# Start addresses of the activation tiles in the three-pass products of a hybrid decoder layer

## The chip, the cores and the metric

The kernel runs on one core of one Trainium2 chip. The metric is device time in microseconds (us) for one execution. Three runs of the kernel before gave 1511.25, 1512.42 and 1514.81 us; the median is 1512.42 us.

## The reference

One decoder layer for 256 tokens of width 2048, all in float32. Cut to what the kernel spends its time on:

```python
h = rms_norm(x, ln1)
proj = h @ w_in                      # 2048 -> 12304 columns: GDN q|k|v, beta, decay, out-gate z,
                                     # MoBA q|k|v, gate A, gate B
y_a = gated_deltanet(...) @ w_branch_a          # 8 heads of 128, chunked delta rule
y_b = moba_attention(q_b, k_b, v_b) @ w_branch_b
merged = sigmoid(gate_a) * y_a + sigmoid(gate_b) * y_b
x = x + merged @ w_out               # 2048 x 2048
h = rms_norm(x, ln2)
u = causal_dwconv(h @ w_up) + bias   # 2048 x 11264
u_gate, u_val = split(u)
x = x + (silu(u_gate) * u_val) @ w_down         # 5632 x 2048
return rms_norm(x, final_norm)
```

## The kernel before

**Three passes.** Every large product is taken in the float32r type, and to keep float32 accuracy each operand is split into a rounded high part and a low rest (`split`, L117 and `low`, L114: ScalarE casts the high part, VectorE subtracts to get the low one). A product is then high x high, plus high x low, plus low x high. The weights come from HBM one 128 x 2048 block at a time (`load_w`), land in `wraw` and are split into `wh` and `wl`, two buffers of each.

**The activation tiles.** For all products but the last the activations are transposed, 128 partitions by 16 (or 8) blocks of the contraction by 256 tokens, and the high and low parts lie side by side in one tile with the shape [128, blocks, 2, 256]:

- `hc` (L220): the normalised input, for the input projection. It stays until the end of the gates; `h2` and `tail` later take the same place in memory (their `tag` is "hc").
- `yca`, `ycb` (L707): the two branches' outputs, 8 blocks each.
- `mc` (L716): the merged branches, for the output projection.
- `h2` (L739): the second normalised input, for the up projection.
- `tail` (L797): no activations; the split weights of the last two blocks of the down projection.

**How they are read.** In `block` (L164 on) TensorE holds 128 columns of `wh` or `wl` and streams the activation tile past them. In wide form, used from the fifth gate chunk on (`WIDE_AT = 4`), one contraction block takes two matmuls, because the high and the low part are read as one row of 512:

```python
main_mm(ps, wh[:, k, :], x[:, k], k == 0, False)                          # 512 columns
main_mm(ps[:, 0, :], wl[:, k, :], x[:, k, 0, :], False, k == kt - 1)      # 256 columns
```

Before that, in narrow form, it takes three matmuls of 256 columns: two with `wh`, one with `wl`. Narrow are the chunks called `gdn`, `z` and `moba` and the first four of `gate`; wide are the other twelve of `gate`, and `br` (from `yca`, `ycb`), `wo` (from `mc`) and `up` (from `h2`). The value projection `ps_v` is the other way round: `hc` is held, in pieces of 128, and 512 columns of `wh` or `wl` stream past. The down projection (`pd`) holds the split activations `ah`, `al` and streams 512 columns of `wh`, `wl` or, for its last two blocks, `tail`. The small product `ps_bd` holds 48 columns of `wb2` and streams `hc`.

**Order.** The Tile framework's scheduler sets the order on each engine when the program is built; weights are loaded on the SP queue, up to four blocks ahead.

**Where the tiles start.** A tile pool gives out addresses in steps of 32 bytes in each partition. In the program that is built, the weights `wh`, `wl` and the activations `ah`, `al` start at a multiple of 64 bytes, and so does `mc`; `hc`, `h2`, `tail`, `yca`, `ycb` and `wb2` start 32 bytes behind one. The rows and pieces within a tile are 512, 1024 or 2048 bytes apart, so that every matmul of a tile starts at the tile's own place.

Of the kernel before, what the change touches and what calls it, by code (L numbers as in the profile page):

```python
# [12 lines left out]
F32R = mybir.dt.float32r  # L13
# [6 lines left out]
P = 128  # L20
T = 256
D = 2048
KD = D // P
H = 8
# [56 lines left out]
def layer_kernel(ctx: ExitStack, tc: tile.TileContext, xT, pos, cst, csel, ceye, vec, convw, ffw, bdv,  # L81
# [7 lines left out]

    def r3(t, b):  # L90
        return t.rearrange("p (a b) -> p a b", b=b)

    def mmg(ps, pairs, start=True, stop=True, **kw):
        n = len(pairs)
        for i, (a, b) in enumerate(pairs):
            pe.matmul(ps, a, b, start=(start and i == 0), stop=(stop and i == n - 1), **kw)  # L96
# [17 lines left out]
    def low(hi, lo, src, eng=None):  # L114
        (eng or dve).tensor_tensor(lo, src, hi.bitcast(F32), op=ALU.subtract)  # L115
# [48 lines left out]
    def block(ps, w, x, kt, k0=0, k1=None):  # L164
        wh, wl = (r3(t, P) for t in w)
        for k in range(k0, k1 or kt):
            if len(ps.shape) == 2:
                for w_, a in ((wh, 0), (wh, 1), (wl, 0)):
                    main_mm(ps, w_[:, k, :], x[:, k, a, :], k == 0 and w_ is wh and a == 0,
                            k == kt - 1 and w_ is wl)  # L170
                continue
            main_mm(ps, wh[:, k, :], x[:, k], k == 0, False)
            main_mm(ps[:, 0, :], wl[:, k, :], x[:, k, 0, :], False, k == kt - 1)
# [43 lines left out]

    hst = ExitStack()
    hp = hst.enter_context(tc.tile_pool(name="hp", bufs=1, side="right"))
    hc = hp.tile([P, KD, 2, T], F32R, name="hc", tag="hc")  # L220
    hh, hl = hc[:, :, 0, :], hc[:, :, 1, :]
    front = ExitStack()
    fk = front.enter_context(tc.tile_pool(name="fk", bufs=1))
# [16 lines left out]
    for i in range(4):  # L240
        scaled(xs[:, 4 * i:4 * i + 4, :], ln1v, 4 * i, hh, hl)
        for b in range(2):
            raw, wh, wl = (t[:, 512 * i:512 * i + 512] for t in wq[b])
            split(wh, wl, raw)
            for k in range(4):
                a = 4 * i + k
                main_mm(ps_q0[:, b], r3(wh, P)[:, k], hh[:, a], a == b == 0, False)
                main_mm(ps_q0[:, b], r3(wh, P)[:, k], hl[:, a], False, False)
                main_mm(ps_q0[:, b], r3(wl, P)[:, k], hh[:, a], False, a == KD - 1)
# [94 lines left out]
    m = m_st.enter_context(tc.tile_pool(name="m", bufs=2, reuse_waits="tile"))  # L344
# [315 lines left out]
    for gr in range(4):  # L660
        h0 = 2 * gr
        qk = []
        for a in range(2):
            ps = chunk(pair(w_moba, 2 * gr + a), hc, KD, "moba")
            t = m.tile([P, 2, T], F32, name=f"qk{a}")
            join(t, ps, R1b)
            qk.append(t)
        if gr % 2 == 0:
            ps = [mmt("ps_v").rearrange("p a b -> p (a b)") for _ in range(2)]
            for q_ in range(4):  # L670
                wh, wl = (r3(t, 512) for t in load_w(w_mv[2 * gr + q_]))
                for i in range(2):
                    s = slice(i * P, (i + 1) * P)
                    for k in range(4):
                        a = q_ * 4 + k
# [28 lines left out]
    yp = y_st.enter_context(tc.tile_pool(name="yp", bufs=1, side="right", reuse_waits="tile"))  # L704
    yc = []
    for t, nm_ in ((ya, "a"), (yb, "b")):
        yc.append(yp.tile([P, H, 2, T], F32R, name="yc" + nm_))  # L707
        for i in range(4):
            s = slice(2 * i, 2 * i + 2)
            act.copy(yc[-1][:, s, 0, :], t[:, s])  # L710
            low(yc[-1][:, s, 0, :], yc[-1][:, s, 1, :], t[:, s], pool)
# [1 line left out]

    m_st = ExitStack()
    m = m_st.enter_context(tc.tile_pool(name="mp", bufs=1, reuse_waits="tile"))
    mc = m.tile([P, KD, 2, T], F32R, name="mc")  # L716
    for c in range(8):
        bts = [yp.tile([P, 2, T], F32, name="bt", bufs=3) for _ in range(2)]
        join(bts[0], chunk(pair(w_ba, c), yc[0], H, "br"), gts[:, c])
# [16 lines left out]
    b = bp.enter_context(tc.tile_pool(name="b", bufs=2, reuse_waits="tile"))  # L736
    x1 = bkeep.tile([P, KD, T], F32, name="x1")
    sqa = b.tile([P, 2, T], F32, name="sqa", bufs=1)
    h2 = hp.tile([P, KD, 2, T], F32R, name="h2", tag="hc")  # L739
    for c in range(8):  # L740
        steps = ((0, 0, KD - 2), (1, 0, 8), (0, KD - 2, KD), (1, 8, KD))
        ps = chunk(pair(w_o, c), mc, KD, "wo", **({} if c else dict(piece=512, steps=steps)))
# [19 lines left out]
    b = bk.enter_context(tc.tile_pool(name="b2", bufs=2, reuse_waits="tile"))  # L762
    ak = bk.enter_context(tc.tile_pool(name="ak", bufs=1, side="right", reuse_waits="tile"))
    acts = ak.tile([P, NF, T], F32, name="acts")
    for c in range(NF):
# [3 lines left out]
        t = b.tile([P, 2, T], F32, name="cvf")  # L769
# [24 lines left out]

    LAST = 4
    wl = {}
    tail = hp.tile([P, 2, 2, 2048], F32R, name="tail", tag="hc")  # L797

    def down(i, n, k, stop=False):
        ah, al, wh, wl_ = wl[k]  # L800
# [105 lines left out]
```

## Time and profile before

| what | us |
|---|---|
| median of three runs | 1512.42 |
| the profiled execution | 1512.97 |
| its span, first to last instruction | 1510.8 |
| TensorE busy | 1487.7 (98%) |
| VectorE busy | 1027.2 (68%) |
| ScalarE busy | 754.6 (50%) |
| up projection, its piece of the chain that ended last | 483.3 |

The profile is one execution. The chain of work that ended last is followed back from the last instruction: its shares say which engine and which line set the end. A matmul's own duration is no measure of pace, since matmuls overlap in the engine's pipeline: the pace is read from the starts of successive matmuls, or from a piece of the chain that is nothing but matmuls, by its length and its count. Below, the pitch is the time from one start to the next. Some matmul records can be missing from a trace, so a count is taken from a short piece where it can be.

### The profile page before, as it was taken

What the parts mean: (1) busy time and instruction counts of PE and PEld (TensorE: products, weight loads), DVE (VectorE), ACT (ScalarE), POOL (GpSimd) and SP (SyncE); (2) the same over time, 40 slices, a digit from 0 to 9 for tenths busy, and PEclk for the clock granted to TensorE, in tenths of its full rate; (3) what the DMA queues carried; (4) which work ended last, traced back from release to release, by engine and by line L of the source; (5) the groups of instructions that cost most, each with busy time, mean ns of one, the idle gap of its engine ahead of it and who ended that gap; (6) DMA issues with size and microseconds to landing.
All of it is one profiled execution on the core that took longest, in us unless ns stands there. A gap on an engine that the chain in (4) does not pass through costs nothing.

```text
span 1510.8 us, 22511 instructions
## 1 busy us (share of the span) xinstructions
PE 1487.7 (98%) x9179; PEld 1337.7 (89%) x9179; DVE 1027.2 (68%) x1453; ACT 754.6 (50%) x1026; POOL 184.9 (12%) x137
## 2 busy tenths in 40 slices
PE   7999999999999999999999999999999999999997
PEld 6999999998998888888888888888888888888886
DVE  7898785886765555777767767667676676555554
ACT  5664464434474444545455555555555554444444
POOL 3001101141221000110101111211111110000000
PEclk9999999999999999999999999999999999999999
DMA  9454444444336553568545555555555554555552
GB/s 312 156 191 165 167 148 171 154 150 165 140 116 219 193 183 126 173 219 307 194 169 195 195 189 190 181 192 196 190 190 181 193 195 167 195 195 195 195 195 84
DMA packets 45639, 276.94 MB, mean 183 GB/s; under 512 B 5504, under 2 KB 6992, under 8 KB 15456
## 3 DMA queue, kind: packets, MB, share of 16 engines
q1 hardware_dynamic: 43712, 270.98, 50.0%
q0 software_dynamic: 960, 2.36, 0.5%
q10 hardware_dynamic: 864, 2.16, 0.4%
q8 instruction: 72, 1.18, 0.3%
q14 instruction: 31, 0.25, 0.0%
HBM read 271.68 MB, written 3.80 MB: 182 GB/s over the span
## 4 chain that ended last, share of the span: by engine, by line
PE 93%; DVE 4%; ACT 1%; issue 1%; DMA 0%; POOL 0%; SPq 0%; DVEq 0%; ACTq 0%
PE ps_up L108 32%; PE pd L96 16%; PE ps_gate L108 11%; PE ps_gdn L108 9%; PE ps_wo L108 6%; PE ps_br L108 5%; PE ps_moba L108 4%; PE ps_z L108 3%; PE ps_v L108 3%; DVE wl L115 2%; ACT wh L118 1%; PE g L96 1%; PE py L545 1%; PE pu L551 1%; DMA wraw<-in_w_gdn 0%
## 5 line engine op out<-in xcount | busy, mean ns | idle before, releaser
L115 DVE TENSOR_TENSOR wl<-wraw,wh 128x1024 fp32r<-128x1024 f32 (+1 forms) x508 | 611.8, 1237 | 255.5 <-ACT wh L118 254.2
L118 ACT CAST wh<-wraw 128x1024 fp32r<-128x1024 f32 (+1 forms) x508 | 502.3, 1033 | 379.3 <-PE ps_up L108 117.5
L108 PE MATMUL ps_up<-h,wh 128*128 128x512 f32 x1408 | 488.6, 390 | 0.0
L108 PE MATMUL ps_up<-h,wl 128*128 128x256 f32 x1408 | 397.0, 282 | 0.0
L108 PEld LDWEIGHTS ps_up<-h,wh 128*128 128x128 f32 x1408 | 264.4, 188 | 55.4
L108 PEld LDWEIGHTS ps_up<-h,wl 128*128 128x128 f32 x1408 | 266.1, 189 | 0.1
L108 PE MATMUL ps_gate<-hc,wh 128*128 128x512 f32 (+1 forms) x640 | 179.6, 347 | 0.0
L108 PE MATMUL ps_gdn<-hc,wh 128*128 128x256 f32 x768 | 143.7, 287 | 8.9 <-ACT wh L118 6.2
L108 PE MATMUL ps_gate<-hc,wl 128*128 128x256 f32 x512 | 144.6, 282 | 0.8 <-DVE wl L115 0.8
L778 POOL TENSOR_TENSOR acts<-sg,cvf 128x256 f32<-128x256 f32 x44 | 80.8, 1836 | 423.3 <-ACT sg L777 423.3
L108 PEld LDWEIGHTS ps_gdn<-hc,wh 128*128 128x128 f32 x768 | 122.1, 194 | 10.3 <-ACT wh L118 6.5
L96 PE MATMUL pd<-wl,ah 128*128 128x512 f32 x336 | 130.8, 389 | 0.0
L96 PE MATMUL pd<-wh,al 128*128 128x512 f32 x336 | 130.8, 389 | 0.0
L108 PEld LDWEIGHTS ps_gate<-hc,wh 128*128 128x128 f32 x640 | 111.4, 188 | 15.1
L108 PE MATMUL ps_gdn<-hc,wl 128*128 128x256 f32 x384 | 110.5, 288 | 1.1 <-DVE wl L115 1.1
L772 ACT ACTIVATE cvf<-unf,ffv 128x256 f32<-128x256 f32 x88 | 48.2, 595 | 104.5 <-DVE unf L199 104.5
L774 DVE SCALAR_TENSOR_TENSOR cvf<-unf,ffv,cvf 128x254 f32<-128x254 f32 (+1 forms) x176 | 77.3, 481 | 32.1 <-ACT cvf L772 31.8
L108 PEld LDWEIGHTS ps_gate<-hc,wl 128*128 128x128 f32 x512 | 96.6, 189 | 1.0 <-DVE wl L115 1.0
L108 PE MATMUL ps_moba<-hc,wh 128*128 128x256 f32 x512 | 93.0, 282 | 0.0
L96 PE MATMUL pd<-wh,ah 128*128 128x512 f32 x336 | 92.8, 391 | 0.0
L108 PE MATMUL ps_wo<-mc,wh 128*128 128x512 f32 x256 | 88.8, 391 | 0.0
L118 ACT CAST ah<-acts 128x256 fp32r<-128x256 f32 x44 | 17.9, 407 | 125.8 <-PE pd L96 116.1
(426 smaller groups left out, 2061.9 us busy)
## 6 DMA issues: line engine op xcount, KB each, us to landing
wraw<-in_w_up SPq DMA_DIRECT2D x88, 1024.0 KB, 4.7
wraw<-in_w_dn SPq DMA_DIRECT2D x44, 1024.0 KB, 4.7
wraw<-in_w_gate SPq DMA_DIRECT2D x32, 1024.0 KB, 4.8
wraw<-in_w_gdn SPq DMA_DIRECT2D x30, 1024.0 KB, 4.8
wraw<-in_w_moba SPq DMA_DIRECT2D x16, 1024.0 KB, 4.8
wraw<-in_w_o SPq DMA_DIRECT2D x16, 1024.0 KB, 4.8
wraw<-in_w_mv SPq DMA_DIRECT2D x8, 1024.0 KB, 4.8
wraw<-in_w_ba SPq DMA_DIRECT2D x16, 512.0 KB, 3.4
```

What stands on the lines that cost most here:

```text
L96: pe.matmul(ps, a, b, start=(start and i == 0), stop=(stop and i == n - 1), **kw)
L108: pe.matmul(ps, a, b, start=start, stop=stop, skip_group_check=True)
L115: (eng or dve).tensor_tensor(lo, src, hi.bitcast(F32), op=ALU.subtract)
L118: act.copy(hi, src)
L545: pe.matmul(py[:, p], ats[p], Tm[:, p], start=True, stop=True)
L551: pe.matmul(pu[:, p], Y[:, p, :], odd(U)[:, p], start=True, stop=True)
L772: act.activation(t[:, j, :], un[:, j, :], AF.Identity, scale=w[:, 2:3], bias=w[:, 3:4])
L774: dve.scalar_tensor_tensor(t[:, j, d:], un[:, j, :T - d], w[:, 2 - d:3 - d], t[:, j, d:], op0=ALU.mult, op1=ALU.add)
L778: pool.tensor_tensor(acts[:, c, :], sg, t[:, 1, :], op=ALU.mult)
```

## The change

Each of the tiles is made 128 elements (512 bytes) longer, and the activations begin some elements into it, by a new helper:

```diff
+    def operand(tp, name, kt, off, tag=None):
+        t = tp.tile([P, kt * 2 * T + 128], F32R, name=name, tag=tag or name)
+        return t[:, off:off + kt * 2 * T].rearrange("p (k a t) -> p k a t", a=2, t=T)
...
-    hc = hp.tile([P, KD, 2, T], F32R, name="hc", tag="hc")
+    hc = operand(hp, "hc", KD, 8, "hc")
...
-        yc.append(yp.tile([P, H, 2, T], F32R, name="yc" + nm_))
+        yc.append(operand(yp, "yc" + nm_, H, 4 if nm_ == "a" else 32))
...
-    mc = m.tile([P, KD, 2, T], F32R, name="mc")
+    mc = operand(m, "mc", KD, 2)
...
-    h2 = hp.tile([P, KD, 2, T], F32R, name="h2", tag="hc")
+    h2 = operand(hp, "h2", KD, 12, "hc")
...
-    tail = hp.tile([P, 2, 2, 2048], F32R, name="tail", tag="hc")
+    tail = hp.tile([P, 2 * 2 * 2048 + 128], F32R, name="tail", tag="hc")[:, :8192].rearrange(
+        "p (a b c) -> p a b c", a=2, b=2)
```

Counted in the two built programs, the start of what the matmuls read, in bytes behind a multiple of 64:

| tile | before | changed | read by |
|---|---|---|---|
| `hc` | 32 | 0 | gdn, z, moba, gate (streamed), ps_v (held) |
| `yca` | 32 | 48 | br, first half |
| `ycb` | 32 | 32 | br, second half |
| `mc` | 0 | 8 | wo |
| `h2` | 32 | 16 | up |
| `tail` | 32 | 32 | pd, last two blocks |
| `wh`, `wl`, `ah`, `al` | 0 | 0 | everywhere |

Other tiles in the same pools move by multiples of 512 bytes and keep their place against 64. On all five engines the two programs hold the same instructions in the same order, with the same shapes and the same waits; no instruction is added, removed or moved.

## Rows read from the trace of the kernel before

**Rows 1.** Page, part 1: busy us, share of the span, instruction count.
```profile
PE 1487.7 (98%) x9179; PEld 1337.7 (89%) x9179; DVE 1027.2 (68%) x1453; ACT 754.6 (50%) x1026; POOL 184.9 (12%) x137
```
**Rows 2.** Chain that ended last: share of the span by engine, tile and line.
```profile
by line: PE ps_up L108 32.3%; PE pd L96 15.9%; PE ps_gate L108 11.1%; PE ps_gdn L108 8.8%; PE ps_wo L108 5.9%; PE ps_br L108 4.6%; PE ps_moba L108 3.9%; PE ps_z L108 3.0%; PE ps_v L108 3.0%; DVE wl L115 2.0%; issue 0.8%; ACT wh L118 0.7%; P
```
**Rows 3.** Stretches: us; busy PE, PEld, DVE, ACT, POOL; granted clock; DMA share; GB/s.
```profile
30.00:400.00 370.00, 367.97 (x2928) 356.33 (x2926) 292.01 (x564) 182.47 (x238) 57.52 (x57) 1.00 0.46 164
...
780.00:1258.00 478.00, 478.00 (x2759) 423.76 (x2759) 332.94 (x435) 251.74 (x349) 79.40 (x43) 1.00 0.53 190
```
**Rows 4.** Pieces of the chain in order of time: start us, us, what, count.
```profile
681.18 88.75 PE ps_wo L108 x512
...
776.52 483.26 PE ps_up L108 x2788
```
**Rows 5.** Timeline of TensorE, value projection: start us, us, matmul, count.
```profile
257.22 0.63 PE L108 MATMUL ps_v<-wh,hc 128*128 128x512 f32 x2
...
259.32 0.40 PE L108 MATMUL ps_v<-wh,hc 128*128 128x512 f32 x1
```
**Rows 6.** Timeline of TensorE, end of the down projection.
```profile
1486.31 1.52 PE L96 MATMUL pd<-wh,ah 128*128 128x512 f32 x6
1487.67 0.39 PE L96 MATMUL pd<-wl,ah 128*128 128x512 f32 x1
...
1489.52 0.39 PE L96 MATMUL pd<-wl,ah 128*128 128x512 f32 x1
...
1491.38 0.40 PE L96 MATMUL pd<-wl,ah 128*128 128x512 f32 x1
```
**Rows 7.** Pieces of the chain: narrow chunks, and the product with 48 held columns.
```profile
28.55 3.63 PE ps_bd L96 x32
...
105.33 11.20 PE ps_z L108 x96
...
327.39 8.63 PE ps_moba L108 x74
...
415.52 9.19 PE ps_gate L108 x78
```
**Rows 8.** Groups of matmuls by shape: count, busy us, mean ns of one.
```profile
L108 PE MATMUL ps_up<-h,wh 128*128 128x512 f32 x1408 | 488.6, 390 | 0.0
...
L108 PE MATMUL ps_gdn<-hc,wh 128*128 128x256 f32 x768 | 143.7, 287 | 8.9 <-ACT wh L118 6.2 <-DVE hc L204 2.6
...
L108 PE MATMUL ps_gate<-hc,wh 128*128 128x512 f32 x384 | 133.2, 390 | 0.0
...
L108 PE MATMUL ps_moba<-hc,wh 128*128 128x256 f32 x512 | 93.0, 282 | 0.0
...
L108 PE MATMUL ps_gate<-hc,wh 128*128 128x256 f32 x256 | 46.5, 282 | 0.0
L108 PE MATMUL ps_z<-hc,wh 128*128 128x256 f32 x256 | 45.9, 281 | 0.0
...
L108 PE MATMUL ps_br<-yca,wh 128*128 128x512 f32 x128 | 44.7, 390 | 0.0
...
L108 PE MATMUL ps_v<-wh,hc 128*128 128x512 f32 x128 | 41.1, 399 | 0.0
```
**Rows 9.** TensorE, start of the kernel: us, busy (count), granted clock, DMA share, GB/s.
```profile
20.00:23.00 3.00, 3.00 (x16) 0.50 0.93 329
```
**Rows 10.** Timeline of TensorE in that stretch.
```profile
22.42 0.63 PE L108 MATMUL ps_gdn<-hc,wh 128*128 128x256 f32 x2
...
23.06 0.63 PE L108 MATMUL ps_gdn<-hc,wh 128*128 128x256 f32 x2
```
**Rows 11.** VectorE groups of the first convolution: count, busy us, mean ns.
```profile
L420 DVE SCALAR_TENSOR_TENSOR kq<-un,cwv,kq 128x253 f32<-128x253 f32 x16 | 7.2, 472 | 0.0
L420 DVE SCALAR_TENSOR_TENSOR kq<-un,cwv,kq 128x255 f32<-128x255 f32 x16 | 7.1, 473 | 0.7 <-ACT kq L418 0.7
L420 DVE SCALAR_TENSOR_TENSOR kq<-un,cwv,kq 128x254 f32<-128x254 f32 x16 | 7.0, 473 | 0.0
```

## The prediction

> **What bounds the kernel now.** I read the busy shares first, then the chain that ended last, then the starts of single matmuls. TensorE is busy for 98% of the span [rows 1], and the chain is TensorE almost throughout: the up projection alone is 32.3% of it, the down projection 15.9%, the gates 11.1% [rows 2]. Over the up projection TensorE has no idle time at the full granted clock, 1.00, which is 2.4 GHz, while VectorE is busy for 333 of 478 us, ScalarE for 252, and the DMA engines for 53% [rows 3]. So in the long stages the end is set by the pitch of the matmuls, and whatever the change does to the pitch passes into the time in full, in both directions: the feeding engines have a quarter or more to spare.
>
> The change touches no instruction, order or wait. All that is left is the address at which an operand starts, so the question is whether the pitch depends on it. The rows say that it does, a little, and not everywhere.
>
> At 2.4 GHz one column takes 0.417 ns: 256 columns 106.7 ns, 512 columns 213.3. The measured pitches are longer. At the start of the kernel the granted clock is 0.50, that is 1.2 GHz [rows 9], and three narrow matmuls take 23.06 - 22.42 = 0.64 us, 213 ns each [rows 10], which is 256 columns at 1.2 GHz with nothing on top. So the excess at full clock is no fixed cost of an instruction; something supplies columns slightly too slowly once the array runs at full speed. Its size in the different stages, with the places against 64 bytes from the table in the section on the change:
>
> - pd with everything at 0: six matmuls of 512 columns in 1487.67 - 1486.31 = 1.36 us, 226.7 ns each [rows 6].
> - pd once six of every eight matmuls stream `tail`, at 32: eight in 1491.38 - 1489.52 = 1.86 us, 232.5 ns each [rows 6].
> - ps_v, which holds `hc` at 32 and streams weights at 0: nine in 259.32 - 257.22 = 2.10 us, 233.3 ns each [rows 5].
> - up, wide, streaming `h2` at 32: 483.26 / 2788 = 173.3 ns, that is 346.7 per pair of a 512 and a 256 [rows 4].
> - wo, wide, streaming `mc` at 0: 88.75 / 512 = 173.3 ns, also 346.7 per pair [rows 4].
> - narrow, streaming `hc` at 32: 11.20 / 96 = 116.7 in z, 8.63 / 74 = 116.6 in moba, but 9.19 / 78 = 117.8 in a gate chunk of the same form [rows 7].
> - ps_bd, also 256 columns of `hc` at 32, but with only 48 columns held: 3.63 / 32 = 113.4 [rows 7].
>
> Per 256 columns this is 113.4 at the best, 115.6 in the wide pairs, 116.7 to 117.8 at the worst. The pitch is lower when fewer columns are held (113.4 against 116.7), and it changes with the place of either operand (226.7 against 232.5 and 233.3). I take this as the streamed operand and the load of the next held one getting in each other's way in the memory, to an extent that depends on how their addresses stand to each other. That is an inference from these rows. The Trainium skill says otherwise: in "SBUF — State Buffer", section "Who interferes with whom", TensorE has two independent read ports, one for the streamed operand and one for the weight load, and never waits on anyone. By that rule no start address matters and the time stays at 1512.4. The trace does not agree with it in pd, where the pitch goes from 226.7 to 232.5 ns with the operand's place.
>
> **The change part by part.** The sum is made against the profiled execution, 1512.97 us; the median of the runs is 0.55 us lower.
>
> *ps_v, `hc` held, 32 to 0.* There are 128 matmuls with `wh` [rows 8] and, by the code, half as many with `wl`: 192. Everything now starts at 0, as in the first stretch of pd, so I take 226.7 for 233.3: 192 x 6.6 ns = 1.3 us less. All of ps_v is on the chain (3.0% of 1510.8 is 45 us, and 192 x 233.3 ns is 44.8) [rows 2]. The other end is no gain.
>
> *Wide chunks.* Places 0 and 32 give the same 346.7 per pair in wo and up, so the wide gates (`hc`, 32 to 0, 384 pairs [rows 8]) get nothing, and `ycb` stays at 32. `h2` goes to 16, `mc` to 8, `yca` to 48: no row shows a matmul operand at such a place. The nearest rows are those of the same pair at 0 and 32, so I take no change. The bounds come from the best and the worst pace of any row, 3 x 113.4 = 340 and 3 x 117.8 = 353 per pair, 6.7 ns either way: up has 1408 pairs [rows 8], plus or minus 9.4 us; wo 256 pairs, 1.7; `yca` 128 pairs [rows 8], 0.9; the wide gates 384 pairs, 2.6.
>
> *Narrow chunks, `hc` streamed, 32 to 0.* With `wh` there are 768 + 512 + 256 + 256 = 1792 [rows 8], with `wl` half as many, 2688 in all, 314 us at 116.7. On the chain are 8.8 + 3.9 + 3.0 = 15.7%, 237 us, and of the gates' 11.1%, 168 us, what the 384 wide pairs (133 us) leave, 35 us: 272 of 314, or 87% [rows 2]. No row shows a narrow stream with both operands at 0. The best pace, 113.4, would give 2688 x 3.3 ns x 0.87 = 7.7 us; the worst, 117.8, would cost 2.6. The wide pairs, the nearest case with a stream at 0 beside one at 32, show no difference; I take none.
>
> *Everything else costs nothing.* ScalarE and VectorE now write the tiles at other places. VectorE's convolution steps, which write 4, 8 and 12 bytes into a row, take 473, 473 and 472 ns [rows 11], so such a place costs VectorE nothing there. ScalarE has no such row; if its writes grew by a tenth, the spare time of the up projection would cover it, and nearly all writes of `h2` and `mc` lie under the matmuls of the stage before. Other tiles move by multiples of 512 bytes.
>
> Sum: 1512.97 - 1.3 = 1511.7 for the profiled execution, 1511.1 against the median. That is less than 0.2% from 1512.4 (3.0 us), about what a measurement of this kernel can tell from no change. All lower ends together give -1.3 - 9.4 - 1.7 - 0.9 - 2.6 - 7.7 = -23.6; all upper ends +9.4 + 1.7 + 0.9 + 2.6 + 2.6 = +17.2.
>
> **The rivals.** *First, `hc` in step with the weights makes the narrow chunks faster.* For it: pd with everything at 0 runs at 113.4 per 256 columns [rows 6]. Against it: wo, also with everything at 0, does not [rows 4]. It gives -7.7 - 1.3 = -9.0, 1503.4. If the new place of `h2` does the same for up, 9.4 more: 1494.0.
>
> *Second, slower: places that are no multiple of 32 upset the up projection's steady pair.* In pd and ps_v a place out of step cost about 6 ns a matmul [rows 5, 6]; up is the longest stage and has no slack on TensorE. At the pace of ps_v and most narrow chunks, 116.7 per 256, the pair takes 350 ns, +3.3 x 1408 = 4.7 us; at 117.8 it is +9.4. wo and `yca` in the same measure add 1.3 to 2.6, ps_v takes 1.3 off: +4.7 to +10.7, that is 1517 to 1523. It decides from a pair of 349.8 on, where 3.1 x 1408 = 4.4 us outweigh ps_v by 3 us. Against it: up and wo differ in place and not in pitch. Also against it is a rule of the Trainium skill, "SBUF — State Buffer", section "Door 1: The DMA port swizzle", that SBUF is read in 16-byte lines and two hits a line suffice: by it 16 and 48 are as good as 32, and `mc` at 8 still has two elements in its first line. The sum would then be that of the forecast; no row here shows a start inside such a line.
>
> *Third, the change does nothing:* ps_v's longer pitch comes from its shape and not from the place of `hc`. Then the time is 1512.4.
>
> **How the numbers follow.** The forecast, pitches as at 0 and 32 and ps_v shorter: 0.30, at 1511.1. The change does nothing: 0.12. Faster through the narrow chunks: 0.20; through up as well: 0.10. Slower: 0.28. So 0.30 faster, 0.42 within 0.2%, 0.28 slower. The forecast's own range is 1509.4 to 1515.4. The range for 8 in 10 takes in the first rival's 1503 and most of the second's, and ends short of both extremes: 1496 to 1525.
>
> **What would show it.** The pitch of each stage, read as above. Right: ps_v at 227, up and wo at 346.7 per pair, z and moba at 116.7. The first rival shows in z and moba near 113.4, or up near 340; the second in up at 350 or more. Wrong altogether would be a pitch beyond the paces seen here, above 353 or below 340 per pair, or a change in VectorE's or ScalarE's times that opens idle time on TensorE.

## The result, and the profile after

| | before | after |
|---|---|---|
| median of the runs, us | 1512.01 (4 runs, 1511.25 to 1514.81) | 1527.81 (4 runs, 1527.12 to 1528.10) |
| the profiled execution, us | 1512.97 | 1527.12 |
| its span, us | 1510.8 | 1525.0 |

The ratio is 1.0105, with a 95% interval of 1.0093 to 1.0117: the change makes the kernel slower by about 15.8 us. That is above the upper end of the predicted range, 1525.

The page of the kernel after answers to [rows 1] with this line (engine, busy time in us, share of the span, instructions):

```profile
PE 1502.6 (99%) x9179; PEld 1336.1 (88%) x9179; DVE 1027.0 (67%) x1453; ACT 754.9 (50%) x1026; POOL 183.5 (12%) x137
```

VectorE and ScalarE are as busy as before to 0.3 us, and TensorE issues the same matmuls; it is only busy for longer. So the place to look is the pitch of the matmuls, stage by stage. The chain that ended last, in the kernel after, gives it (start in us, length in us, what, number of instructions; one line is one unbroken stretch of matmuls):

```profile
17.73 9.34 PE ps_gdn L112 x62
27.07 3.73 PE ps_bd L100 x32
...
104.44 11.31 PE ps_z L112 x96
...
256.16 9.33 PE ps_v L112 x40
...
415.94 9.19 PE ps_gate L112 x78
...
449.81 141.36 PE ps_gate L112 x814
...
684.30 90.45 PE ps_wo L112 x512
...
781.38 492.54 PE ps_up L112 x2788
...
1282.29 235.03 PE pd L100 x1035
```

Two of the lines have their counterpart of before in [rows 4]: up takes 492.54 us where it took 483.26, with the same count, and wo 90.45 where it took 88.75. For z and one narrow gate chunk it is [rows 7]: 11.31 against 11.20, and 9.19 against 9.19. For the wide gates and the down projection the same view of the kernel before has

```profile
449.36 138.81 PE ps_gate L108 x814
...
1268.14 235.03 PE pd L96 x1035
```

A wide pair is two instructions, so up and wo now run at 2 x 492.54 / 2788 = 353.3 ns a pair, the worst pace that the prediction had allowed for, where they ran at 346.7. The wide gates lose 2.55 us over 384 pairs, which is 6.6 ns a pair and so the same pace. The narrow matmuls of z run at 11.31 / 96 = 117.8 ns instead of 116.7. The down projection is unchanged to the last digit. And ps_v did not become faster, as the starts of its single matmuls in the kernel after show (start in us, us, what; lines with x2 hold two matmuls, of which the second's start isn't shown):

```profile
256.23 0.39 PE L112 MATMUL ps_v<-wl,hc 128*128 128x512 f32 x1
256.47 0.63 PE L112 MATMUL ps_v<-wh,hc 128*128 128x512 f32 x2
...
258.33 0.39 PE L112 MATMUL ps_v<-wl,hc 128*128 128x512 f32 x1
```

From the first of these starts to the last are nine matmuls in 2.10 us, 233.3 ns each, as in [rows 5].

Set side by side by the starts of the stages, the profiled executions differ by +1.93 us in the narrow part (from ps_bd to the wide gates), +2.55 in the wide gates, +0.1 in br, +1.70 in wo, +9.28 in up and nothing in the down projection: +15.6 us together, of the 15.8 between the medians. The spans differ by 14.2, because in the profiled execution of the kernel after ps_bd begins 1.48 us earlier, at 27.07 instead of 28.55.

br loses next to nothing although its pitch did change. With `yca` at its new place a pair takes about 350 ns instead of 346.7, by the starts in the trace. But br is not a stage of matmuls alone. The chain of the kernel before, and below it that of the kernel after:

```profile
605.32 8.27 PE ps_br L108 x46
...
614.69 2.24 DVE wl L115
616.98 8.27 PE ps_br L108 x46
```
```profile
608.40 8.30 PE ps_br L112 x46
...
617.81 2.21 DVE wl L119
620.06 8.29 PE ps_br L112 x46
```

Between two pieces of br the chain runs through the splitting of the next weights, and from one piece to the next it is 11.66 us in both kernels. There the pitch is not what sets the time.

### The profile page after: what moved, and what is told of

It is laid out like the page before. It is cut to its first block, busy times and chain, and to the rows that moved or that the text cites. A ratio compares the mean times of both kernels' runs of the same rounds, so it can differ in the third digit from the quotient of the medians.

```text
span 1525.0 us, 22511 instructions
## 1 busy us (share of the span) xinstructions
PE 1502.6 (99%) x9179; PEld 1336.1 (88%) x9179; DVE 1027.0 (67%) x1453; ACT 754.9 (50%) x1026; POOL 183.5 (12%) x137
## 4 chain that ended last, share of the span: by engine, by line
PE 93%; DVE 4%; ACT 1%; issue 1%; DMA 1%; SPq 0%; POOL 0%; DVEq 0%; ACTq 0%
PE ps_up L112 33%; PE pd L100 16%; PE ps_gate L112 11%; PE ps_gdn L112 9%; PE ps_wo L112 6%; PE ps_br L112 5%; PE ps_moba L112 4%; PE ps_z L112 3%; PE ps_v L112 3%; DVE wl L119 2%; ACT wh L122 1%; PE g L100 1%; PE py L549 1%; PE pu L555 1%; DMA xs<-in_xT 1%
## 5 line engine op out<-in xcount | busy, mean ns | idle before, releaser
L112 PE MATMUL ps_up<-h,wh 128*128 128x512 f32 x1408 | 497.9, 398 | 0.0
L112 PE MATMUL ps_up<-h,wl 128*128 128x256 f32 x1408 | 392.9, 279 | 0.0
```

What stands on the lines that cost most here:

```text
L112: pe.matmul(ps, a, b, start=start, stop=stop, skip_group_check=True)
```

## The experiments

Two theories stood at first. *Place:* the pitch depends on where the streamed tile begins. *Layout:* the padding shifts every tile that comes behind it in memory, and that is what counts. Later the question became what a place is counted against. The diffs below are against the changed kernel; where nothing is said, every kernel does the whole computation. A time without an interval is that of one execution, beside executions of the kernel before between 1511.3 and 1512.2 us on the same chips.

### The padding without the offsets

```diff
-    hc = operand(hp, "hc", KD, 8, "hc")
+    hc = operand(hp, "hc", KD, 0, "hc")
...
-    h2 = operand(hp, "h2", KD, 12, "hc")
+    h2 = operand(hp, "h2", KD, 0, "hc")
```

`yca`, `ycb` and `mc` begin at 0 elements in the same way; all tiles keep their 512 bytes more.

> The tiles are 512 bytes longer as in the change, but every one begins at its old place (hc, yca, ycb, h2 and tail 32 bytes behind a multiple of 64, mc at 0). Place theory (the pitch of a stage follows from where its activation tile starts): every pitch as in the kernel before, 346.7 ns per wide pair in up, wo and the gates, 116.7 narrow, time 1511 to 1513. Layout theory (longer tiles and pools moved by 512 bytes are the cause): as in the changed kernel, 353.3 per pair, 117.8 narrow, 1527 to 1528.

Measured: 1510.52 us. The chain of this kernel:

```profile
446.91 138.77 PE ps_gate L112 x814
...
678.64 88.75 PE ps_wo L112 x512
...
773.97 483.26 PE ps_up L112 x2788
```

These are the lengths of before. The offsets do it all, and the layout theory falls.

### One tile at a time

With `h2` alone at its new offset (12 elements), and the others at 0:

> As the padded kernel with old places, but h2 begins 16 bytes behind a multiple of 64, as in the change. Place theory: up 353.3 ns per pair, 1408 x 6.6 = 9.3 us, time 1521; all other stages as before. Theory of a rhythm carried over from stage to stage (up is slow because the stages ahead of it are): up 346.7, time 1512.

Measured: 1516.18 us. Up has become longer, wo is as before, but up is not as long as in the changed kernel. The chain of the kernel with `h2` alone:

```profile
679.60 88.75 PE ps_wo L112 x512
...
775.01 487.90 PE ps_up L112 x2788
```

That is 350.0 ns a pair, where the same tile at the same offset ran at 353.3 in the changed kernel. The reverse, the change with `h2` back at 0:

> The changed kernel with h2 alone back at 32 bytes behind a multiple of 64. Place theory: up back at 346.7 ns per pair, 9.3 us less than the changed kernel, 1518.4; wo stays at 353.3 per pair, the wide gates at 353.3, the narrow chunks at 117.8. Rhythm theory (a run of matmuls keeps a rhythm into which it falls at its entry, the place only limits which): up may also lie at 350 or 353.

Measured: 1518.58 us; up back at 483.25 us for 2788, wo still at 90.45 and the wide gates at 141.36. And `hc` alone at its new offset (8 elements):

> Only hc is moved, as in the change (0 behind a multiple of 64, 64 against the weights modulo 256); yca, ycb, mc, h2 at their old places. Place theory with the pitches of the changed kernel: wide gates 353.3 ns per pair, 384 x 6.4 = 2.5 us; narrow chunks 117.8 instead of 116.9, 2688 x 0.9 x 0.87 = 2.1 us; wo and up 346.7; time 1512 + 4.6 = 1516.6. If a slow rhythm of the gates is carried into the stages behind it: up or wo at 350 or more, 1518 to 1526.

Measured: 1515.41 us; the wide gates at 141.37, z at 11.31, wo at 88.75 and up at 483.26. So a stage is slow only when its own tile has moved, and a slow stage doesn't make the next one slow. In the changed kernel `h2` costs 9.3 us, `hc` about 4.5 and `mc` 1.7. But `h2` alone costs only 4.6 (487.90 against 483.26 us): how much its place costs isn't settled by the place alone. The section on the two rhythms takes that up.

### What the place is counted against

Two kernels with other offsets for all five tiles. First hc 56, yca 88, ycb 120, mc 8 and h2 72 elements:

> Other places, all counted from the place of the weights: hc at 0, yca at 128, ycb at 256, mc at 32, h2 at 64 bytes. If only the place against 64 bytes counts, hc, yca, ycb and h2 are alike (0) and as hc in the changed kernel: 353.3 ns per pair in gates, br and up. If the place against the weights in steps of 128 counts, hc, yca and ycb are as mc was before (0): 346.7, mc at 32 346.7, and h2 at 64 is as hc in the changed kernel: 353.3, up 9.3 us longer. If the place doesn't count, all 346.7.

Measured: 1522.65 us. Then hc 60, yca 72, ycb 80, mc 12 and h2 56:

> Places counted from the weights: hc at 16, yca at 64, ycb at 96, mc at 48, h2 at 0 bytes. Steps of 128: h2 346.7 ns per pair (as mc before), yca 353.3 (as hc in the changed kernel), hc at 16, mc at 48 and ycb at 96 unknown, 340 to 353. Against 64 bytes alone: h2 and yca 353.3, ycb 346.7. If a multiple of 32 is what keeps the short pitch: hc and mc 353.3, all others 346.7.

Measured: 1513.0 us. In the second, up is at 483.26 us, the pace of before, with `h2` 224 bytes behind its old place; the wide gates are at 138.84, and wo at 89.60 for 512, 350.0 a pair. In the first, `h2` lies another 64 bytes further on and up takes 486.36 (348.9 a pair), and the wide gates take 141.46. Against a multiple of 64 both places of `h2` are 0, and they do not run alike: the count against 64 in the table of the change is not what matters.

Then the weights themselves were moved, by a tile of 32 bytes that the pool gives out ahead of all others, with the activations left where the padding alone has them:

```diff
+    shim = keep.tile([P, 8], F32, name="shim")
+    nc.gpsimd.memset(shim, 0.0)
```

> A 32-byte tile ahead of all others moves wh, wl, ah, al and mc to 32 bytes behind a multiple of 64; hc, yca, ycb, h2 and tail keep 32. Against the weights the latter now stand at 0 modulo 64. If the place against the weights counts: narrow chunks near 120 (as with hc at 0 against them), ps_v near 227 instead of 233 per matmul, the last matmuls of pd on tail at 227 instead of 232.5, up and wo 346.7 per pair. If the place in memory alone counts: hc, h2 and ps_v as in the kernel before (116.7, 346.7, 233), and pd, now streaming from 32 throughout, near 232 instead of 227, 5 to 6 us longer.

Measured: 1530.31 us, slower than the change itself. The chain of this kernel:

```profile
107.11 11.52 PE ps_z L112 x96
...
261.11 9.10 PE ps_v L112 x40
...
454.73 141.47 PE ps_gate L112 x814
...
689.62 88.75 PE ps_wo L112 x512
...
784.95 492.54 PE ps_up L112 x2788
...
1285.81 234.64 PE pd L100 x1035
```

No activation has an odd place in memory here, and yet up runs at 353.3 ns a pair and z at 11.52 / 96 = 120.0 ns a matmul. What has changed is the distance between the two operands: it was 32 bytes for `hc`, `h2` and `tail`, and is 0 now. At the same time ps_v (9.10 us for 40, 227.5 ns each) and the stretch of pd that streams `tail` (226.7 instead of [rows 6]'s 232.5) became faster. And wo, for which both `mc` and the weights moved by 32 bytes, kept its 88.75. So the place counts as the distance from the held tile to the streamed one: moving both together changed nothing, and moving one alone changed the pitch, in up for the worse and in ps_v for the better. The first of the two kernels with other offsets says the same from the other side. There `hc` was moved by 224 bytes and the weights were not, so that the distance is 256 bytes; z takes 11.52 us for 96 matmuls, the wide gates 141.46 for 814 and ps_v 9.10 for 40, as with the weights moved by 32 (141.47 for the gates).

### The period of the distance

A sweep that gave every few chunks of up another distance, by lengthening the weight tiles by 32 elements (128 bytes) and beginning at another element of them. It took for granted that the pattern repeats every 128 bytes:

```diff
-        wh, wl = into or [wpool.tile([P, 2048], F32R, name=t, tag=t) for t in ("wh", "wl")]
+        o_ = woff[0]
+        wh, wl = into or [wpool.tile([P, 2048 + 32], F32R, name=t, tag=t)[:, o_:o_ + 2048] for t in ("wh", "wl")]
```

> Activation tiles at their old places. The weights' tiles are 128 bytes longer, and in the up projection they begin, four chunks (128 matmuls) at a time, at another place, so that h2 stands 0, 8, 16, 24, 40, 48, 56, 64, 80, 96 and 112 bytes (modulo 128) behind them. If the place of the two operands against each other sets the pitch, with several rhythms possible at some places: per pair 346.7 to 353.3 ns at 0, 353.3 at 8, 347 at 16, 350 at 48, 349 to 353.3 at 64, 350.0 or 353.3 at 80, 350 at 96; 24, 40, 56 and 112 not seen so far. If the place of the streamed tile in memory alone counts: 346.7 throughout, since h2 doesn't move.

Measured: 1522.84 us. All stretches of up lay between 348 and 353 ns a pair, and stages that the sweep left alone became longer: pd took 238.37 us for 1035 and wo 90.07 for 512. The second half of it, with other distances and with the narrow stages:

> The same with other places in another order in up (104, 112, 88, 64, 72, 48, 16, 0, 4, 20, 36), and also in the narrow chunks (0, 8, 16 and so on to 120, one chunk each), the value projection (0) and the gates. Places against each other: ps_v at 227 to 229 ns a matmul instead of 233.3, narrow at 0 near 119.9, at 8 to 120 within 113.3 to 120; places that both sweeps visit give the same pitch or one of two that differ by 3 to 7 ns per pair. Place in memory alone: ps_v 233.3, narrow 116.7, up 346.7.

Measured: 1524.99 us, and as confused. Neither is a clean sweep: with tiles lengthened by 128 bytes, successive buffers of the weights lie 128 bytes apart modulo 256, and that they no longer run alike says that the period is not 128. The third lengthens them by 64 elements (256 bytes):

> Activation tiles at their old places; the weights' tiles are 256 bytes longer instead of 128, so that all their buffers stand alike modulo 256. In up h2 stands 0, 16, 64, 80, 96, 128, 160, 192, 208, 224 and 240 bytes (modulo 256) behind the weights, four chunks each; ps_v's weights are moved by 32 bytes so that hc stands at 0 against them. If what counts repeats every 256 bytes: pd back at 226.7 ns a matmul and wo at 346.7 per pair (with the tiles 128 bytes longer they were at 230 and 352), the stretches at 0 at 346.7 or 353.3, at 80 at 350.0 or 353.3; ps_v 227 to 229. If it repeats only every 512 bytes or more: pd and wo stay at 230 and 352. If some place of h2 gives the pace of pd, 340 per pair, it shows here.

Measured: 1513.59 us. pd and wo are back at 235.03 and 88.75, so that with 256 bytes the buffers run alike again. The windows of this kernel, for the up projection alone, at four distances (window, its length, busy us and number of TensorE matmuls, weight loads, VectorE, ScalarE, granted clock, DMA share, GB/s):

```profile
816.00:856.00 40.00, 40.00 (x228) 34.95 (x227) 2.50 (x4) 1.72 (x3) 1.00 0.51 185
1040.00:1080.00 40.00, 40.00 (x232) 35.22 (x231) 2.73 (x4) 1.75 (x3) 1.00 0.51 185
1085.00:1125.00 40.00, 40.00 (x228) 34.73 (x227) 2.21 (x4) 1.73 (x3) 1.00 0.52 184
1130.00:1170.00 40.00, 40.00 (x233) 35.12 (x232) 2.42 (x4) 1.73 (x3) 1.00 0.51 185
```

TensorE is never idle and the clock is full in all four; in 40 us it starts 228 matmuls at the distances 16 and 192, and 232 or 233 at 160 and 208. In the same kernel `hc` as the held operand of ps_v has the distance 0:

```profile
255.78 0.39 PE L112 MATMUL ps_v<-wl,hc 128*128 128x512 f32 x1
...
259.18 0.39 PE L112 MATMUL ps_v<-wl,hc 128*128 128x512 f32 x1
```

15 matmuls in 3.40 us, 226.7 ns each: the gain that the prediction had expected of the change, at the place that the change did not have.

The fourth sweep, over the narrow chunks:

> Activation tiles at their old places, weights' tiles 256 bytes longer; each narrow chunk takes another place of hc against its weights: 32, 0, 16, 48, 64 and so on in steps of 16 to 240 (gdn and z), 240, 208, 160, 48, 16, 112, 144, 176 (moba); the wide gates take 32, 48, 112, 144, 176, 240, 208, 160, 8, 24, 40, 56, one chunk each; ps_v 0. If the narrow chunks follow the place modulo 256 as the wide pairs do: at 0 119.9 ns, at 32 116.7 to 117.8, at 64 117.8, and the pace of pd, 113.4, at some place would show a gain of up to 7.7 us. The wide gates at 32, 160, 208, 240: 346.7 per pair as up had there; at 48 350; at 8 353.3.

Measured: 1514.91 us. At most distances 116.7 to 120 ns a matmul, at 192 113.6 to 114.0 in the three stretches of the one chunk there. The wide gates, one chunk each, ran at 346.7 to 347.1 ns a pair at 32, 160, 208 and 240 and at 350.0 at 48, as expected; at 8 it was 352 for the expected 353.3.

Put together, with the distance from the held operand to the streamed one modulo 256 bytes (ns, the mean between starts in stretches without other matmuls; several figures where different stretches or kernels showed them; 128 bytes longer tiles are left out):

| distance | wide pair | narrow |
|---|---|---|
| 0 | 346.7, 353.3 | 120 |
| 8 | 352, 353.3 | |
| 16 | 347, 353.3 | 113.3, 116.7, 118.7, 120 |
| 24 | 351 | |
| 32 | 346.7 | 116.7, 117.8 |
| 40 | 351 | |
| 48 | 350.0, 351 | 116.7 |
| 56 | 350 | |
| 64 | 348.9, 353.3 | 113.5, 117.8 |
| 80 | 349.3, 350.0, 353.3 | 118.1 |
| 96 | 350.0 | 120 |
| 112 | 349 | 119.4, 119.9 |
| 128 | 351 | 119.2 |
| 144 | 353 | 119.7 |
| 160 | 346.7 | 117.4, 118.3 |
| 176 | 353 | 118.7 |
| 192 | 353.3 | 113.4, 117.8 |
| 208 | 346.7 | 117.9 |
| 224 | 353.3 | 118.4 |
| 240 | 346.7 | 118.4 |

Before, `hc`, `yca`, `ycb`, `h2` and `tail` had the distance 32 and `mc` 0. The change gives `hc` 64, `yca` 48, `ycb` 160, `mc` 8 and `h2` 80. `ycb`'s stage kept its 347. In ps_v the roles are changed round: there `hc` is the held tile and the weights are streamed, and the same places give 224 before, 192 in the changed kernel, and 0 where the two stand alike.

### One place, two rhythms

Distance 80 gave 350.0 in one kernel and 353.3 in another. Two kernels have a few matmuls too many in the up projection, ahead of the first matmul of every fourth chunk, which disturb the regular alternation (their sums are overwritten by the matmul that follows). `n_`, `held` and `times` differ from chunk to chunk:

```diff
+            if k == 0 and kick:
+                n_, held, times = kick.pop()
+                for _ in range(times):
+                    pe.matmul(ps.rearrange("p a t -> p (a t)")[:held, :n_], wh[:, k, :held],
+                              x[:, k].rearrange("p a t -> p (a t)")[:, :n_],
+                              start=True, stop=False, skip_group_check=True)
```

With all tiles at their old distances:

> Old places; in the up projection, ahead of every fourth pair of chunks, one to three extra matmuls of another length (256, 512, 128, 64, 2 x 256, 32, 256 with 48 held, 16, 3 x 256, 4 columns) go into the accumulator that the next matmul overwrites. They add about 3 us in all. Place theory: between them every stretch runs at 346.7 ns per pair. Rhythm theory: stretches behind different extras run at different pitches, among 340, 346.7, 350 and 353.3.

Measured: 1513.02 us, every stretch at 346.7. With `h2` at 80:

> The same extra matmuls, with h2 at 16 bytes behind a multiple of 64 and all other tiles at their old places. Place theory: one pitch for the whole of up, 350.0 ns per pair as with h2 moved alone. Rhythm theory: stretches at 350.0 and at 353.3 (as in the changed kernel), perhaps others, and a pitch changes only at an extra matmul or another interruption.

Measured: 1521.43 us. The chain of the kernel with extra matmuls and `h2` at 80 (L180 is the extra matmul):

```profile
815.35 45.22 PE ps_up L112 x256
860.57 0.23 PE ps_up L180
860.81 44.80 PE ps_up L112 x256
905.61 0.06 PE ps_up L180
905.67 45.27 PE ps_up L112 x256
...
1178.10 44.80 PE ps_up L112 x256
...
1222.91 45.32 PE ps_up L112 x256
```

45.22 us for 256 is 353.3 ns a pair and 44.80 is 350.0. Between two extra matmuls the pitch stays; it changes only at one, and not at every one. So the distance says which rhythms are possible, and what came ahead of a stretch says which of them it falls into; at 32 a wide pair showed only one, and none of ten disturbances dislodged it.

No extra matmuls are needed for it. In every kernel the up projection begins with 28 matmuls, then come four others (`R`, for the normalisation), and then the rest. The changed kernel, from the third of these matmuls with 512 columns to the last, and below it the kernel with `h2` alone, from the fourth on to the last (start in us, us, what):

```profile
776.16 0.40 PE L112 MATMUL ps_up<-h,wh 128*128 128x512 f32 x1
...
780.01 0.39 PE L112 MATMUL ps_up<-h,wh 128*128 128x512 f32 x1
...
780.36 1.03 PE L100 MATMUL R<-sq,ones 128*128 128x256 f32 x4
```
```profile
770.10 0.40 PE L112 MATMUL ps_up<-h,wh 128*128 128x512 f32 x1
...
773.63 0.40 PE L112 MATMUL ps_up<-h,wh 128*128 128x512 f32 x1
...
773.98 1.02 PE L100 MATMUL R<-sq,ones 128*128 128x256 f32 x4
```

Eleven pairs in 3.85 us are 350.0 ns each, ten in 3.53 us are 353. So ahead of `R` the changed kernel ran at 350.0 and the kernel with `h2` alone at 353.3, and behind it each ran at the other's pitch to the end of up, the one at 353.3 and the other at 350.0. The 4.6 us between them are a matter of which rhythm up fell into behind these four matmuls.

### The best distances

The sweeps point to 192 for the narrow chunks, 0 for ps_v and `tail`, and 32 for the wide ones:

```diff
+    NARROW, VALUE, WIDE = 24, 8, 0
+    woff = [NARROW]
...
-        wh, wl = into or [wpool.tile([P, 2048], F32R, name=t, tag=t) for t in ("wh", "wl")]
+        o_ = woff[0]
+        wh, wl = into or [wpool.tile([P, 2048 + 64], F32R, name=t, tag=t)[:, o_:o_ + 2048] for t in ("wh", "wl")]
```

> Activation tiles at their old places; the weights' tiles are 256 bytes longer and begin 96 bytes in for the narrow chunks (hc then stands at 192 against them modulo 256), 32 bytes in for ps_v (hc at 0), 0 for the wide chunks (as before); tail begins at 0 against ah and al. Place theory: narrow chunks 113.6 ns instead of 116.9, 2688 x 3.3 x 0.87 = 7.7 us less; ps_v 227 to 229 instead of 233.3, 0.9 to 1.2 us less; tail 0.3 us less; wide as before: 1512 - 9 = 1503. If the short pitch at 192 was a rhythm that one stretch happened on: narrow at 117 to 118 for the most part, 1510 to 1512.

Measured: 1509.30 us (median of 11 runs, 1509.09 to 1511.80) beside 1511.52 for the kernel before (15 runs), a ratio of 0.9986 with an interval of 0.9977 to 0.9995. This is faster than both kernels, by 2.2 us, but far from the 1503 expected. The chain of this kernel:

```profile
33.05 21.44 PE ps_gdn L112 x189
...
84.93 19.67 PE ps_gdn L112 x167
104.59 11.31 PE ps_z L112 x96
...
256.10 9.10 PE ps_v L112 x40
...
326.74 8.40 PE ps_moba L112 x74
...
1265.64 234.67 PE pd L100 x1035
```

ps_v and pd deliver. The narrow chunks do so in part: 21.44 / 189 = 113.4 in one stretch, 19.67 / 167 = 117.8 in the next, at the same distance. 192 is another place with two rhythms, which the sweep, with three short stretches at it, had not shown. Nor is the short pitch a mark of 192: in the kernel with `hc` 60 elements in, at the distance 16, one stretch of gdn took 5.44 us for 48 matmuls, 113.3 each, and in the changed kernel, at 64, one of moba took 4.20 for 37, 113.5. No distance was found at which all narrow chunks keep it.

## Why the prediction was wrong

**Right:** what bounds the kernel in its long stages, and so that there a change of the pitch passes into the time in full. Of the 15.8 us, 15.6 are found in the pitches of the stages, and order and waits are the same. It doesn't hold in br, where the splitting of the weights stands between the pieces. Right too was that the pitch depends on how the addresses of the streamed and the held operand stand to each other; that it is the load of the held one that gets in the way is the prediction's reading, and no run separates it from others. The Trainium skill ("SBUF — State Buffer", section "Who interferes with whom") has TensorE's two read ports independent and TensorE never waiting on anyone. These runs don't agree with that, if it is taken to make start addresses free: by moving the weights alone by 32 bytes, up went from 346.7 to 353.3 ns a pair.

**The step that failed: "Places 0 and 32 give the same 346.7 per pair in wo and up", and so no change for `h2`, `mc` and `yca`.** Two places that give the same pitch were taken as a sign that the pitch of a wide pair hardly depends on the place. It does: of the distances in the table, more are slower than 346.7 than not, and none is faster. The kernel before stood at one of the fast ones. The upper bound, 353 a pair from the worst narrow row, was exact: +9.28 for +9.4 in up, +1.70 for +1.7 in wo. For `yca` it was too high, with 0.1 in br for 0.9: the pair took about 350, and even that did not reach the time, because br waits for its weights. So the right price was in the sum as an upper end, and the value taken, no change, was wrong. That 353 was the measured pitch was in part luck: it was taken from a narrow row, and with `h2` alone at the same distance up ran at 350.0.

**"The wide gates get nothing (32 to 0)", and none for the narrow chunks.** This failed in the place itself. I counted it against a multiple of 64 bytes, with the held and the streamed tile each by itself; against the weights modulo 256, `hc` went from 32 to 64. That cost +2.55 for the upper end's 2.6 in the wide gates, and +1.93 for 2.6 in the narrow part, where a gate chunk had the slower 117.8 already. Even at the distance 0 that I took it to have, the forecast would have failed: 353.3 and 120.0 with moved weights.

**ps_v, -1.3.** The mechanism was right and the place wrong: where `hc` and the weights stand alike it takes 226.7, as said, but `hc` stood 64 bytes from them and ps_v kept its 233.3.

**The best pace, "lower when fewer columns are held".** This rested on one piece of ps_bd with 48 held columns, at 113.4. With the offsets at 0 and the padding alone, the same piece took 3.74 us for 32, 116.9 a matmul, while 128 held columns ran at 113.4 in the last experiment. The row showed one of two paces at the same addresses, and nothing on the held columns. Nor has ps_bd one place to compare: its held pieces are 48 columns, 192 bytes, apart, so that what is said of the rows and pieces of all tiles, that each matmul starts at the tile's own place, doesn't hold for `wb2`.

**The range.** All upper ends together gave +17.2, which is 1529.6 against the median; the range was cut at 1525, as though the ends came up independently of each other. They had one cause in common, that a moved tile leaves the distance which suits it, and three of the five (up, wo, the wide gates) came up whole. The second rival, slower because such places upset the steady pair, had the right sign and the right rows. It was priced at up to 1523 and given 0.28. Against it stood that up and wo differ in place and not in pitch, the failed step again, and a rule of the Trainium skill ("SBUF — State Buffer", section "Door 1: The DMA port swizzle") on 16-byte lines, by which 16 and 48 are as good as 32. The runs don't bear that out: 48 gives 350.0 for a pair, and 16 gives 353.3 in one kernel and 347 in another.

**What stays open.** Which part of the memory makes the two operands wait for each other, and what decides at the entry of a stretch into which rhythm it falls, isn't shown. So it is open, too, why up fell behind the four `R` matmuls into 353.3 in the changed kernel and into 350.0 with `h2` alone; shown is that both rhythms exist at this distance in either kernel, and that one stray matmul can switch them.

## What to carry to other kernels

When TensorE is the bound and its matmuls run close to their columns' time, the start of the streamed tile against that of the held one is a parameter of the kernel, worth a per cent here. So read the pitch of each long stage before and after anything that moves a tile, padding included. Two places with the same pitch don't show that places are harmless; look for the distance between both operands, and at a pitch that a disturbance doesn't change. When the unknown terms of a sum share one cause, their ends come up together, and the range must reach to their sum.

## What the runs showed of the hardware

- With 128 held columns in float32r, the pitch depends on the distance between the starts of the held and the streamed tile, with a period of 256 bytes at the distances where this was tried (128 isn't one): 346.7 to 353.3 ns for a pair of 512 and 256 columns, 113.4 to 120 for 256, 226.7 to 233.3 for 512.
- Many steady pitches are 3.33 ns apart, which is 8 periods of 2.4 GHz: 113.3, 116.7 and 120.0 for 256 columns are 272, 280 and 288 periods, and 346.7, 350.0 and 353.3 for a pair 832, 840 and 848. Others lie between, and those that could be followed repeat over several matmuls, with a whole that fits the same steps: 117.8 in z of the changed kernel is three matmuls in 353.3 ns (848 periods), and 348.9 for a pair with `h2` at 64 is three pairs in 1046.7 (2512 periods). No run shows why.
- At some distances (80 and 192 among them) the same instructions at the same addresses run in one of two rhythms, and keep it until something breaks the regular alternation; at 32 a wide pair showed only 346.7.
